# Joining 24 of 32 work units into twelve of 8 MB in an instance-norm kernel

## The chip, the cores and the metric

The kernel runs on one core of a Trainium2 chip. A core has a matrix engine (TensorE, PE), a vector engine (VectorE, DVE), an activation engine (ScalarE, ACT), GpSimd (POOL) and a synchronising engine (SyncE, SP), which run side by side, each in the order of its own instructions. Data moves between the memory outside (HBM) and the on-chip memory (SBUF, 128 partitions) by DMA: an engine issues a transfer on its queue, and 16 DMA engines carry it, each a part of the rows. The metric is the device time of one run in microseconds. Three runs of the kernel before gave 626.78, 626.83 and 626.91 us; the median is 626.83.

## The reference

```python
def reference(x, gamma):            # x: (4, 8, 16, 256, 256) f32, gamma: (8, 16)
    mu = x.mean(axis=(3, 4), keepdims=True)
    var = ((x - mu) ** 2).mean(axis=(3, 4), keepdims=True)
    x_norm = (x - mu) / np.sqrt(var + 1e-5)
    out = x_norm * gamma[None, :, :, None, None]
```

There are 4 x 8 x 16 = 512 channels of 65536 numbers, 134 MB in and as many out. Each channel is normalised by its own mean and variance and scaled by its gamma. The input is read once and the output written once.

## The kernel before

The input is one long run of numbers, cut into 32 units of 4 MB (16 channels each). A unit is a tile of 128 partitions by 8192 numbers; a channel lies in 8 neighbouring partitions (S = 8), and each partition's row of 32 KB is contiguous in HBM. Six slots (AHEAD = 6) of 4 MB hold units; unit u uses slot u % 6.

At the start (L51 to L57) a small store writes into the output ("touch"), gamma is loaded, and six loads are issued: units 1 and 3 on ACT's queue, the others on SP's. Setup then builds, on GpSimd, a 128 x 128 matrix (navg) that sums over the 8 partitions of a channel and divides by -65536, and, with TensorE and VectorE, a column of gammas per unit (g_col).

The loop over units (L104) is unrolled, in this order for each unit:

- L106, VectorE: the sum of each row into st. L107, ScalarE: the square of each element (its output goes to junk) and the sum of the squares into st.
- L115, TensorE: one matmul of navg with the two columns of st, into PSUM: minus the mean and minus the mean square, in each partition of the channel.
- L116 (VectorE), L120 (ScalarE, square root), L124 and L126 (VectorE): the variance, its root, the reciprocal and the scale.
- L135, VectorE: the tile is normalised in place. In unit 0 alone, ScalarE does 3/8 of the row (L132).
- L139, ScalarE's queue: the store of the tile. L141, SP's queue: the load of unit u + 6 into the same slot, which waits until that store has landed.

The order on every queue is the program's order. All stores, and the loads of units 1 and 3, are on ACT's queue (q10 in the profile); all other loads on SP's (q1). The program tracks dependencies by parts of a tile: in unit 0, VectorE and ScalarE write two parts of one tile at the same time.

Of the kernel before, what the change touches and what calls it, by code (L numbers as in the profile page):

```python
# [1 line left out]

# [4 lines left out]

F32 = mybir.dt.float32
U8 = mybir.dt.uint8
ALU = mybir.AluOpType  # L10
ACTF = mybir.ActivationFunctionType
AX = mybir.AxisListType


@with_exitstack
def kernel(
    ctx: ExitStack,
    tc: tile.TileContext,
    x: bass.AP,
    gamma: bass.AP,  # L20
    out: bass.AP,
):
    nc = tc.nc
    B, G, C, H, W = x.shape
    P = nc.NUM_PARTITIONS
    HW = H * W
    n_ch = B * G * C
    S = 8
    K = P // S
    F = HW // S  # L30
    U = n_ch // K
    NG = (G * C) // K
    AHEAD = 6
    assert HW % S == 0 and (G * C) % K == 0

    xv = x.rearrange("b g c h w -> (b g c h w)").rearrange("(u p f) -> u p f", p=P, f=F)
    ov = out.rearrange("b g c h w -> (b g c h w)").rearrange("(u p f) -> u p f", p=P, f=F)
    gv = gamma.rearrange("g c -> (g c)")

    data = ctx.enter_context(tc.tile_pool(name="data", bufs=1))  # L40
    singles = ctx.enter_context(tc.tile_pool(name="singles", bufs=1))
    psum = ctx.enter_context(tc.tile_pool(name="psum", bufs=4, space=bass.MemoryType.PSUM))
    ctx.enter_context(tc.manual_schedule())

    slots = [data.tile([P, F], F32, name=f"xt{i}") for i in range(AHEAD)]

    def load(u, queue):
        queue.dma_start(out=slots[u % AHEAD][:], in_=xv[u])  # L48


    g_row = singles.tile([1, G * C], F32, name="g_row")  # L51
    touch = singles.tile([16, 128], F32, name="touch")
    nc.vector.memset(touch[:], 0.0)  # L53
    nc.gpsimd.dma_start(out=ov[0][0::S, 0:128], in_=touch[:])  # L54
    nc.gpsimd.dma_start(out=g_row[:], in_=gv[None, :])  # L55
    for u in range(AHEAD):
        load(u, nc.scalar if u in (1, 3) else nc.sync)  # L57

    eps_t = singles.tile([P, 1], F32, name="eps_t")
    nc.gpsimd.memset(eps_t[:], 1e-5)  # L60
    one = singles.tile([1, 1], F32, name="one")
    nc.gpsimd.memset(one[:], 1.0)
    navg = singles.tile([P, K, S], F32, name="navg")
    nc.gpsimd.memset(navg[:], -1.0 / HW)  # L64
    nc.gpsimd.affine_select(  # L65
        out=navg[:], in_=navg[:], pattern=[[-S, K], [0, S]], compare_op=ALU.is_ge,
        fill=0.0, base=0, channel_multiplier=1,
    )
    nc.gpsimd.affine_select(  # L69
        out=navg[:], in_=navg[:], pattern=[[S, K], [0, S]], compare_op=ALU.is_ge,  # L70
        fill=0.0, base=S - 1, channel_multiplier=-1,
    )
    navg_w = navg[:].rearrange("p k s -> p (k s)")
    root_eps = singles.tile([P, 1], F32, name="root_eps")
    nc.scalar.activation(out=root_eps[:], in_=eps_t[:], func=ACTF.Sqrt)  # L75
    g_rep = singles.tile([1, NG, K, S], F32, name="g_rep")
    g_ps = psum.tile([P, NG], F32, name="g_ps", bufs=1)
    g_col = singles.tile([P, NG], F32, name="g_col")

    nc.vector.tensor_copy(  # L80
        out=g_rep[:],
        in_=g_row[:].rearrange("o (n k) -> o n k", n=NG).unsqueeze(3).to_broadcast([1, NG, K, S]),
    )
    for n in range(NG):
        nc.tensor.matmul(  # L85
            out=g_ps[:, n : n + 1],
            lhsT=g_rep[:, n].rearrange("o k s -> o (k s)"),
            rhs=one[:],
            start=True, stop=True,
        )  # L90
    nc.vector.tensor_copy(out=g_col[:], in_=g_ps[:])  # L91

    junk = singles.tile([P, F], U8, name="junk")

    st = singles.tile([P, U, 2], F32, name="st")
    nvar = singles.tile([P, U], F32, name="nvar")
    std = singles.tile([P, U], F32, name="std")
    rstd = singles.tile([P, U], F32, name="rstd")
    scale = singles.tile([P, U], F32, name="scale")

    shift = singles.tile([P, 1], F32, name="shift")

    squares = []
    for u in range(U):  # L104
        t = slots[u % AHEAD]
        nc.vector.reduce_sum(out=st[:, u, 0:1], in_=t[:], axis=AX.X)  # L106
        square = nc.scalar.activation(  # L107
            out=junk[:], in_=t[:], func=ACTF.Square, accum_out=st[:, u, 1:2],
        )
        if u:  # L110

            tc.declare_no_dep(square.ins, squares[-1].ins, reason="junk, ordered by the root between")
        squares.append(square)
        ps = psum.tile([P, 2], F32, name="ps")
        nc.tensor.matmul(out=ps[:], lhsT=navg_w, rhs=st[:, u], start=True, stop=True)  # L115
        nc.vector.tensor_scalar(  # L116
            out=nvar[:, u : u + 1], in0=ps[:, 0:1], scalar1=ps[:, 0:1],
            scalar2=ps[:, 1:2], op0=ALU.mult, op1=ALU.add,
        )
        nc.scalar.activation(  # L120
            out=std[:, u : u + 1], in_=nvar[:, u : u + 1], func=ACTF.Sqrt,
            bias=eps_t[:], scale=-1.0,
        )
        nc.vector.reciprocal(out=rstd[:, u : u + 1], in_=std[:, u : u + 1])  # L124
        g = u % NG
        nc.vector.tensor_mul(  # L126
            out=scale[:, u : u + 1], in0=rstd[:, u : u + 1], in1=g_col[:, g : g + 1],
        )
        cut = F * 5 // 8 if u == 0 else F
        if cut < F:  # L130
            nc.vector.tensor_mul(out=shift[:], in0=ps[:, 0:1], in1=scale[:, u : u + 1])  # L131
            nc.scalar.activation(  # L132
                out=t[:, cut:], in_=t[:, cut:], func=ACTF.Identity, bias=shift[:], scale=scale[:, u : u + 1],
            )
        nc.vector.tensor_scalar(  # L135
            out=t[:, :cut], in0=t[:, :cut], scalar1=ps[:, 0:1], scalar2=scale[:, u : u + 1],
            op0=ALU.add, op1=ALU.mult,
        )
        nc.scalar.dma_start(out=ov[u], in_=t[:])  # L139
        if u + AHEAD < U:  # L140
            load(u + AHEAD, nc.sync)  # L141


# [1 line left out]
_INS = ['x', 'gamma']  # L145
_OUTS = [((4, 8, 16, 256, 256), 'float32')]


# [23 lines left out]
```

## Time and profile before

| what | value |
|---|---|
| median of three runs | 626.83 us |
| span of the profiled execution, first to last instruction | 625.2 us (its own device time is not given apart from the span) |
| VectorE busy | 441.8 us, 71% |
| ScalarE busy | 241.8 us, 39% |
| TensorE busy | 21.4 us, 3% |
| HBM traffic | 134.22 MB read, 134.23 MB written, 429 GB/s over the span |
| first load issued / first packet | 0.81 / 1.82 us |
| last load lands | 585.5 us |
| last store issued / landed | 600.6 / 624.3 us |

The page gives the busy time of each engine, the span in 40 slices with the DMA engines' share of busy time, the DMA queues with their packets, and groups of instructions with their mean duration and what ended the idle time before them. A packet is one row's contiguous bytes, or the 4 B that marks a transfer as complete on one DMA engine. Groups are named by line of the kernel, engine, operation and tiles.

### The profile page before, as it was taken

Reading aid. Unit: us, or ns where it says so; the run is one execution under the profiler, and the core shown is the slowest. Engines: PE = TensorE matmul, PEld = TensorE weight load, DVE = VectorE, ACT = ScalarE, POOL = GpSimd, SP = SyncE. Lnnn points to the kernel's source line nnn. Section 1 sums busy time; section 2 is a strip of 40 time slices with the busy share of each in tenths; the row PEclk is TensorE's granted clock in tenths of the full one; section 3 lists DMA queues with packets and bytes.
Section 4 is the critical chain, followed back from the end, with each engine's and each line's share of the span. In section 5 each row is a group of like instructions: output and inputs, shape, how many; then the busy total and the mean of one; then the engine's idle time right before and its main releaser. Section 6 shows DMA issues by size and latency. Waiting matters only on the chain.

```text
span 625.2 us, 635 instructions
## 1 busy us (share of the span) xinstructions
PE 21.4 (3%) x80; PEld 19.5 (3%) x80; DVE 441.8 (71%) x164; ACT 241.8 (39%) x99; POOL 2.4 (0%) x11
## 2 busy tenths in 40 slices
PE   0200000000000000000000000000000000000000
PEld 0200000000000000000000000000000000000000
DVE  0589999998776687666786767867668676687730
ACT  0464444444443244432344423444224442244400
POOL 1000000000000000000000000000000000000000
DMA  8999999999999999999999999999999999999998
GB/s 370 436 407 432 436 436 436 436 436 430 423 436 434 434 428 434 434 436 436 436 436 428 426 436 436 432 430 434 434 436 436 436 436 421 432 436 434 434 430 367
DMA packets 9282, 268.46 MB, mean 429 GB/s; under 512 B 1072, under 2 KB 1088, under 8 KB 1088
## 3 DMA queue, kind: packets, MB, share of 16 engines
q10 hardware_dynamic: 4896, 142.61, 52.9%
q1 hardware_dynamic: 4320, 125.83, 46.8%
q0 software_dynamic: 64, 0.01, 0.0%
q14 instruction: 2, 0.02, 0.0%
HBM read 134.22 MB, written 134.23 MB: 429 GB/s over the span
## 4 chain that ended last, share of the span: by engine, by line
another core or an unknown queue 61%; DMA 17%; DVE 15%; SPq 1%; PE 1%; issue 0%; ACT 0%
DMA xt<-in_x_dram 10%; DVE st L106 10%; DMA out_dram<-xt 8%; DVE xt L135 5%; SPq L48 1%; PE ps L115 1%; ACT std L120 0%; DVE nvar L116 0%; DVE rstd L124 0%; DVE scale L126 0%; DVE shift L131 0%
## 5 line engine op out<-in xcount | busy, mean ns | idle before, releaser
L106 DVE TENSOR_REDUCE st<-xt 128x1 f32<-128x8192 f32 x32 | 277.9, 8684 | 102.2 <-DMA xt<-in_x_dram 102.2
L107 ACT ACTIVATE junk<-xt 128x8192 uint8<-128x8192 f32 x32 | 225.0, 7030 | 272.0 <-DMA xt<-in_x_dram 233.8
L135 DVE TENSOR_SCALAR xt<-xt,ps,scale 128x8192 f32<-128x8192 f32 (+1 forms) x32 | 144.0, 4500 | 1.1
L120 ACT ACTIVATE std<-nvar,eps_t 128x1 f32<-128x1 f32 x32 | 9.4, 295 | 79.4 <-DVE nvar L116 79.4
L115 PE MATMUL ps<-st,navg 128*128 128x2 f32 x64 | 17.8, 348 | 557.3 <-DVE st L106 557.3
L115 PEld LDWEIGHTS ps<-st,navg 128*128 128x128 f32 x64 | 16.0, 310 | 559.1 <-issue 546.2
L116 DVE TENSOR_SCALAR nvar<-ps 128x1 f32<-128x1 f32 x32 | 9.2, 286 | 23.8 <-PE ps L115 23.8
L124 DVE RECIPROCAL rstd<-std 128x1 f32<-128x1 f32 x32 | 5.2, 163 | 11.6 <-ACT std L120 11.6
L80 DVE COPY g_rep<-g_row 1x1024 f32<-1x1024 f32 x1 | 0.7, 681 | 14.4 <-DMA g_row<-in_gamma_dram 14.4
L107 ACT ACTIVATION_READ_ACCUMULATOR junk<-xt 128x1 f32 x32 | 6.0, 186 | 0.0
L126 DVE TENSOR_TENSOR scale<-rstd,g_col 128x1 f32<-128x1 f32 x32 | 5.1, 158 | 1.1
L85 PE MATMUL g_ps<-one,g_rep 1*128 1x1 f32 x16 | 3.5, 347 | 16.3 <-DVE g_rep L80 16.3
L85 PEld LDWEIGHTS g_ps<-one,g_rep 1*128 1x128 f32 x16 | 3.5, 326 | 16.3 <-issue 16.3
L132 ACT ACTIVATE xt<-xt,shift,scale 128x3072 f32<-128x3072 f32 x1 | 2.9, 2947 | 0.7 <-DVE shift L131 0.7
L91 DVE COPY g_col<-g_ps 128x8 f32<-128x8 f32 x1 | 0.2, 167 | 3.7 <-PE g_ps L85 3.7
L75 ACT ACT_TABLE_LOAD x1 | 1.3, 1283 | 1.7 <-PEq L156 1.7
L53 DVE MEMSET touch<- 16x128 f32 x1 | 0.2, 165 | 0.9 <-PEq L156 0.9
L54 POOL DMA_DIRECT2D out_dram<-touch x1 | 0.6, 617 | 0.8 <-DVE touch L53 0.8
L55 POOL DMA_DIRECT2D g_row<-in_gamma_dram x1 | 0.5, 487 | 0.0
L65 POOL TENSOR_SCALAR_AFFINE_SELECT navg<-navg 128x128 f32<-128x128 f32 x1 | 0.4, 400 | 0.1
L69 POOL TENSOR_SCALAR_AFFINE_SELECT navg<-navg 128x128 f32<-128x128 f32 x1 | 0.4, 399 | 0.1
L64 POOL MEMSET navg<- 128x128 f32 x1 | 0.2, 230 | 0.0
(8 smaller groups left out, 1.0 us busy)
## 6 DMA issues: line engine op xcount, KB each, us to landing
out_dram<-xt ACTq DMA_DIRECT2D x32, 4096.0 KB, 62.5
xt<-in_x_dram SPq DMA_DIRECT2D x30, 4096.0 KB, 38.5
xt<-in_x_dram ACTq DMA_DIRECT2D x2, 4096.0 KB, 31.7
out_dram<-touch POOLq DMA_DIRECT2D x1, 8.0 KB, 9.3
g_row<-in_gamma_dram POOLq DMA_DIRECT2D x1, 0.5 KB, 13.5
```

The source lines that it names most:

```text
L48: queue.dma_start(out=slots[u % AHEAD][:], in_=xv[u])
L75: nc.scalar.activation(out=root_eps[:], in_=eps_t[:], func=ACTF.Sqrt)
L85: nc.tensor.matmul(out=g_ps[:, n : n + 1], lhsT=g_rep[:, n].rearrange("o k s -> o (k s)"), rhs=one[:], start=True, stop=True,)
L106: nc.vector.reduce_sum(out=st[:, u, 0:1], in_=t[:], axis=AX.X)
L107: square = nc.scalar.activation(out=junk[:], in_=t[:], func=ACTF.Square, accum_out=st[:, u, 1:2],)
L115: nc.tensor.matmul(out=ps[:], lhsT=navg_w, rhs=st[:, u], start=True, stop=True)
L116: nc.vector.tensor_scalar(out=nvar[:, u : u + 1], in0=ps[:, 0:1], scalar1=ps[:, 0:1], scalar2=ps[:, 1:2], op0=ALU.mult, op1=ALU.add,)
L120: nc.scalar.activation(out=std[:, u : u + 1], in_=nvar[:, u : u + 1], func=ACTF.Sqrt, bias=eps_t[:], scale=-1.0,)
L124: nc.vector.reciprocal(out=rstd[:, u : u + 1], in_=std[:, u : u + 1])
L126: nc.vector.tensor_mul(out=scale[:, u : u + 1], in0=rstd[:, u : u + 1], in1=g_col[:, g : g + 1],)
L132: nc.scalar.activation(out=t[:, cut:], in_=t[:, cut:], func=ACTF.Identity, bias=shift[:], scale=scale[:, u : u + 1],)
L135: nc.vector.tensor_scalar(out=t[:, :cut], in0=t[:, :cut], scalar1=ps[:, 0:1], scalar2=scale[:, u : u + 1], op0=ALU.add, op1=ALU.mult,)
```

## The change

The 32 units become 20: four of 4 MB, twelve of 8 MB, four of 4 MB (sizes, in halves of 4 MB). An 8 MB unit has 128 rows of 64 KB, 32 channels, and a channel lies in 4 partitions (S = 4). The six slots become three tiles of two half-slots each (pairs); an 8 MB unit takes a whole pair, a 4 MB unit a half. The memory taken is the same. Each unit is still loaded by one transfer and stored by one.

An 8 MB unit is summed and squared half by half (two reductions and two squares of 8192 numbers), its two matmuls add up in PSUM, and it is normalised by one instruction over 16384 numbers. There are two averaging matrices and two gamma columns, for S = 8 and S = 4. A load goes out after the store of the last unit that still held part of its place: the loads of units 16 and 17 follow store 13, those of units 18 and 19 follow store 14. The first loads are those of units 0 to 4.

```diff
-    S = 8
-    K = P // S
-    F = HW // S
-    AHEAD = 6
+    F = 8192
+    HALVES = 6
+    ENDS = 4
+    sizes = [1] * ENDS + [2] * ((n_half - 2 * ENDS) // 2) + [1] * ENDS
+    starts = [sum(sizes[:i]) for i in range(len(sizes))]
+    def rows(flat, u):
+        n = sizes[u] * P * F
+        lo = starts[u] * P * F
+        return flat[lo : lo + n].rearrange("(p f) -> p f", p=P)
-    slots = [data.tile([P, F], F32, name=f"xt{i}") for i in range(AHEAD)]
+    pairs = [data.tile([P, 2 * F], F32, name=f"xt{i}") for i in range(HALVES // 2)]
+    def home(u):
+        at = starts[u] % HALVES
+        return pairs[at // 2], (at % 2) * F
     def load(u, queue):
-        queue.dma_start(out=slots[u % AHEAD][:], in_=xv[u])
+        t, c = home(u)
+        src = rows(x_flat, u)
+        n = sizes[u] * F
+        step = n
+        for k in range(0, n, step):
+            queue.dma_start(out=t[:, c + k : c + k + step], in_=src[:, k : k + step])
-    for u in range(AHEAD):
+    first = [u for u in range(len(sizes)) if starts[u] + sizes[u] <= HALVES]
+    for u in first:
         load(u, nc.scalar if u in (1, 3) else nc.sync)
+    for S in (8, 4):
+        K = P // S
+        w = singles.tile([P, K, S], F32, name=f"navg{S}")
...
     for u in range(U):
-        t = slots[u % AHEAD]
-        nc.vector.reduce_sum(out=st[:, u, 0:1], in_=t[:], axis=AX.X)
+        t, c = home(u)
+        S = 8 // sizes[u]
+        halves = range(sizes[u])
+        for h in halves:
+            part = t[:, c + h * F : c + (h + 1) * F]
+            col = starts[u] + h
+            nc.vector.reduce_sum(out=st[:, col, 0:1], in_=part, axis=AX.X)
+            square = nc.scalar.activation(
+                out=junk[:], in_=part, func=ACTF.Square, accum_out=st[:, col, 1:2],
+            )
         ps = psum.tile([P, 2], F32, name="ps")
-        nc.tensor.matmul(out=ps[:], lhsT=navg_w, rhs=st[:, u], start=True, stop=True)
+        for h in halves:
+            nc.tensor.matmul(
+                out=ps[:], lhsT=navg[S], rhs=st[:, starts[u] + h],
+                start=h == 0, stop=h == sizes[u] - 1,
+            )
...
+        step = sizes[u] * F
+        for k in range(0, sizes[u] * F, step):
+            n = min(step, cut - k)
+            nc.vector.tensor_scalar(
+                out=t[:, c + k : c + k + n], in0=t[:, c + k : c + k + n], scalar1=ps[:, 0:1],
+                scalar2=scale[:, u : u + 1], op0=ALU.add, op1=ALU.mult,
+            )
+            nc.scalar.dma_start(out=dst[:, k : k + step], in_=t[:, c + k : c + k + step])
-        if u + AHEAD < U:
-            load(u + AHEAD, nc.sync)
+        for v in range(len(first), U):
+            need = starts[v] + sizes[v] - HALVES
+            if starts[u] < need <= starts[u] + sizes[u]:
+                load(v, nc.sync)
```

## The prediction

> **What bounds the kernel now.** I read the page's slices first, then its queues and issues, then the engines' groups, and last the DMA view of short windows and the chain at the end.
>
> ```profile
> span 625.2 us, 635 instructions
> ...
> DMA  8999999999999999999999999999999999999998
> ...
> DMA packets 9282, 268.46 MB, mean 429 GB/s; under 512 B 1072, under 2 KB 1088, under 8 KB 1088
> ...
> q10 hardware_dynamic: 4896, 142.61, 52.9%
> q1 hardware_dynamic: 4320, 125.83, 46.8%
> ...
> L106 DVE TENSOR_REDUCE st<-xt 128x1 f32<-128x8192 f32 x32 | 277.9, 8684 | 102.2 <-DMA xt<-in_x_dram 102.2
> L107 ACT ACTIVATE junk<-xt 128x8192 uint8<-128x8192 f32 x32 | 225.0, 7030 | 272.0 <-DMA xt<-in_x_dram 233.8
> L135 DVE TENSOR_SCALAR xt<-xt,ps,scale 128x8192 f32<-128x8192 f32 (+1 forms) x32 | 144.0, 4500 | 1.1
> ...
> out_dram<-xt ACTq DMA_DIRECT2D x32, 4096.0 KB, 62.5
> xt<-in_x_dram SPq DMA_DIRECT2D x30, 4096.0 KB, 38.5
> ```
>
> The two data queues fill 99.7% of the 16 DMA engines' time: q1 (SP's, the loads) and q10 (ACT's, all stores and two loads). VectorE, the next busiest, idles 102 us for loads. So only two things change the time: what a packet costs, and whether a DMA engine ever has nothing to do.
>
> Packet starts in the trace price both. On one engine, 32 KB packets start 1209.5 ns apart, a 512 B packet holds the engine 23 ns, a 4 B one (a transfer's completion mark, one per engine) 6 ns. A line through 512 B and 32 KB has 4.5 ns that does not depend on size.
>
> Next, how queues share an engine: the DMA view of a window (7.1 to 9.55 us) in which a small transfer runs on q0.
>
> ```profile
> DMA packets 48, 1.06 MB, mean 431 GB/s; under 512 B 0, under 2 KB 16, under 8 KB 16
> ## 3 DMA queue, kind: packets, MB, share of 16 engines
> q1 hardware_dynamic: 16, 0.52, 49.5%
> q10 hardware_dynamic: 16, 0.52, 49.5%
> q0 software_dynamic: 16, 0.01, 1.1%
> ```
>
> Each queue put through 16 packets, one per engine, though q0's have 512 B and the others 32 KB. The turn is a packet, not a number of bytes; the 4 B marks take turns of their own too. Last, the end of the chain and of the timeline:
>
> ```profile
> 547.05 38.49 DMA xt<-in_x_dram
> ...
> 596.03 4.55 DVE xt L135
> ```
>
> ```profile
> 585.57 8.69 DVE L106 TENSOR_REDUCE st<-xt 128x1 f32<-128x8192 f32 x1 [4.33 <-DMA xt<-in_x_dram]
> ...
> 600.62 0.34 ACTq L139 DMA_DIRECT2D out_dram<-xt  x1
> ```
>
> The last load lands at 585.54. Four stores of 4 MB are then left, 9.66 us each (they land at 595.2, 604.9, 614.6 and 624.3). The last is issued at 600.6, while the one ahead of it still runs until 614: 13 us of cover, and the DMA never stops.
>
> **The change part by part.**
>
> *Packets.* Twelve 8 MB units move 128 rows of 64 KB each way: 8 packets per engine in place of 16. That removes 12 x 2 x 8 = 192 packets per engine, at 4.5 ns: 0.86 us; 24 fewer completion marks at 6 ns: 0.14 us. Gain 1.0 us. A 64 KB packet is then 2 x 1209.5 - 4.5 = 2414.5 ns. No row shows one: bounds are a packet cost of 8 ns (the recorded length of a 32 KB packet, 1213, less its bytes), a gain of 1.7, and none at all. The starts are nearest, so 1.0. The Trainium skill ("DMA: Bandwidth & Descriptors", Why small descriptors are slow) gives some 3 cycles per packet, 3.5 ns at its 850 MHz; an estimate from that page makes the gain 0.8 us, where the trace's row makes it 1.0.
>
> *Issues.* 24 fewer, at 0.33 us on SP and 0.34 on ACT; hidden before (both queues held transfers), so nothing.
>
> *Setup.* A second averaging matrix on GpSimd (a memset and two selects, 0.23 + 0.40 + 0.40 us) ends before 5 us and is needed at 31. The second gamma column adds to VectorE a copy of 512 (at most the 0.68 of the 1024 one) and one of 0.17, to TensorE 4 matmuls at 0.22, with waits some 2 us from 20.06; the first load lands at 22.75. If that cover fails, unit 0 is at most 1 us late, and its store waits behind a load on q10 until about 41 anyway. Nothing.
>
> *Chain of a unit.* From landing to store issue a 4 MB unit takes 15.05 us (585.57 to 600.62). An 8 MB unit starts only when all of it has landed: a second reduction (+8.61) and a normalisation of 16384 in place of 8192 (+4.29, by the slope between the 5120 and 8192 forms, 2.94 and 4.55): 28.0. Squares (2 x 7.2 on ACT) lie beside the reductions; the first half's matmul beside the second's reduction; the second half's costs what the matmul cost before. Per 8 MB that is 28.0 in place of 30.1, so VectorE gains.
>
> *Buffers.* With both queues on 64 KB packets, a transfer takes 8 pairs of turns, 8 x 4.83 = 38.6 us. A pair of half-slots goes through load 38.6, chain 28.0, store 38.6 and about 4 us of marks, landings (0.4) and first packets (1.0 after issue, from 0.81 to 1.82 at the start): 109 of the 3 x 38.6 = 116 us that three pairs allow. Nothing lost in the middle, with 7 us to spare.
>
> *The ends, where sizes mix.* Here a 64 KB packet on one queue alternates with a 32 KB one on the other, 2.41 against 1.21, so the queue with big rows gets two thirds. At the head the big one is a load (unit 4, beside stores 0 and 1): loads run ahead, harmless, since VectorE is at units 0 to 3 until 81. At the tail it is the stores: loads 16 to 19 are small, stores 14 and 15 big. I walked each engine's turns through the program by the rules above (alternate packets, marks a turn, landing 0.4, first packet 1.0 after issue, chains 15.05 and 28.0). For the kernel before the walk gives load 4 at 62.5 (trace 62.4), the last load at 585.3 (585.5) and the span 625.0 (625.2). For the change:
>
> - The load of unit 15 lands at 506.9. Before, 4 loads (of 32) were left at 508; now also 4, so no change so far.
> - Load 16 against store 14: 8 x (2.41 + 1.21) = 29.0 us, to 535.5. Equal packets would have taken 19.4.
> - Store 15 is ready in time (506.9 + 28.0 + 1.0 = 536.0), so load 17 pays the same: to 564.5.
> - Loads 18 and 19 against stores 16 and 17, small on both sides: 19.4 each, to 583.9 and 603.3. The last load is 18 us later than before.
> - Then only stores 18 and 19 are left. Store 18 runs to 613.0. Unit 19 lands at 603.7, its store is issued at 618.75 and starts at 619.7.
>
> The DMA stands idle from 613.0 to 619.7: 6.7 us. What is late is the last unit's chain, whose cover of 13 us is gone. Sum: 625.2 - 1.0 + 6.7 = 630.9 us of span. The median of the three runs, 626.83, lies 1.6 above the span shown (which leaves out launch and end), taken as fixed: **632.5 us**, slower by 0.9%.
>
> The walk steps by packets: if the 8 MB chain takes 29, 30 or 32 us, or first packets take 1.3 to 2.0 us after issue, store 15 comes later, some load packets go unopposed, and the span is 1.2 to 3.6 us lower; tried over these values it lay from 627.2 to 631.7. Random lateness of packets, as in the trace's odd 1.23 to 1.3 us ones near 100 us, adds up to 0.7. With the 0.2 us by which the walk falls short before, and the 1.6, that is 629 to 633.8 for this case's time.
>
> **Rivals.**
>
> *The engines share by bytes once packets differ (not slower).* A 64 KB row might be served as two turns of 32 KB. The place is the tail from 507 on: load 16 takes 19.4, the last load ends at 586.3, the last store is issued at 601.8 with store 18 running to 613, and only the packet gain is left: 626.83 - 1.0 = 625.8. It decides as soon as the last load ends before 596.5 (16.5 ahead of 613.0). Against it: 16 packets of 512 B for 16 of 32 KB. For it: no row shows a packet over 32 KB between two queues.
>
> *The rows are cut into 32 KB pieces (the change does not do what it says).* Then only the marks are saved: 626.7. The trace shows no 64 KB row, so neither for nor against, save that the 32 KB rows went whole.
>
> *Large packets stream more slowly.* Each 1% on a 64 KB packet costs 24 x 19.32 x 0.01 = 4.6 us; with the tail's loss, 637 at 1%; without, 630. For it: the first stores beside loads (40 to 44 us) fell to 369 GB/s; against: all later mixing held 431 to 436. The Trainium skill ("DMA: Bandwidth & Descriptors", Latency and other measured facts, on HBM row pitch at large powers of two) has rates falling as the pitch of rows grows, from 207 GB/s a direction at 512 KiB to 103 at 4 MiB. The change doubles the pitch from 32 to 64 KB, still below its list; no run shown here tests it.
>
> *Three pairs starve the DMA in the middle.* It needs a chain over 37 us where the sum has 28.0; at 40, the walk ends at 639.7, 641 for the median. Nothing in the rows adds 9 us to the chain.
>
> **How the numbers follow.** Alternation at the tail: 0.72, since the sharing rule is shown by three packet sizes but not at 64 KB. Bytes: 0.10. Cut rows: 0.07. Slower packets: 0.06. Starving: 0.05. A difference of 0.2% is 1.25 us, about what a measurement of this kernel tells from none. Of the first, 0.03 could end within it (a long chain), the rest is slower: 0.69 + 0.06 + 0.05 = 0.80. Same: 0.03, cut rows 0.07, and half of bytes (625.8 is just inside 625.58): 0.15. Faster: the rest of bytes, 0.05. The likeliest case's own range is 629 to 633.8 and holds about 0.69; reaching down to cut rows and bytes, at 625.7, takes it to 0.86.
>
> **What would show it.** The page should have 5120 data packets, 640 marks and the 66 others: 5826 in place of 9282 (8898 if rows are cut). Window 510 to 560: q10 moves twice q1's bytes if turns are packets, equal bytes otherwise. The last landing of a load: about 603.7 (586 by bytes). The DMA's slices just before the end: a gap of 5 to 7 us, and the chain of waits ending in the last load, its reduction, its normalisation and its store. Middle slices stay full, and 64 KB packets start 2.41 us apart. The prediction is wrong if q10's share at the tail is one half, if store 15 is late enough to let loads run alone, or if the middle shows gaps.

## The result and the profile after

The changed kernel takes 637.56 us (median of 4 runs, 633.88 to 638.31), the kernel before 626.87 (626.78 to 627.34). The ratio is 1.0157, 95% interval [1.0132, 1.0182]: slower by 1.6%, where 632.5 and slower by 0.9% was forecast, with 633.8 as the upper end. The profiled execution took 638.2 us for a span of 636.5, so 1.7 us lie around the span, as with the kernel before.

The page of the changed kernel, in lines that answer to those shown before:

```profile
span 636.5 us, 556 instructions
...
DMA  9999999999999999999999999999999999999966
GB/s 375 441 404 428 437 404 412 461 416 441 445 408 457 408 449 441 416 449 408 449 416 449 453 408 449 408 449 457 412 449 408 449 428 426 457 395 426 430 289 266
DMA packets 5827, 268.48 MB, mean 422 GB/s; under 512 B 688, under 2 KB 704, under 8 KB 704
...
L135 DVE TENSOR_REDUCE st<-xt 128x1 f32<-128x8192 f32 x32 | 276.8, 8681 | 149.3 <-DMA xt<-in_x_dram 149.3
```

The rows did become packets of 64 KB: 5827 in all, 5826 forecast. VectorE works 11 us less than before (430.8 us busy, 441.8 before) and waits 47 us more for loads (149.3, 102.2 before). Up to the last two slices the DMA engines look full; those two, 289 and 266 GB/s, hold most of the loss. Two stretches of the end, columns as in the profile's table by stretches (start and end, length in us, busy time and instructions of PE, its weight loads, DVE, ACT and POOL, granted clock, DMA share, GB/s; packets are counted where they start, so a share can pass 1):

```profile
613.00:625.00 12.00, 0.56 (x2) 0.50 (x2) 10.30 (x5) 3.87 (x3) 0.00 (x0) 1.00 0.27 113
625.00:635.00 10.00, 0.00 (x0) 0.00 (x0) 0.00 (x0) 0.00 (x0) 0.00 (x0) 1.00 0.98 419
```

The timeline of the same end:

```profile
590.09 8.69 DVE L135 TENSOR_REDUCE st<-xt 128x1 f32<-128x8192 f32 x1 [9.79 <-DMA xt<-in_x_dram]
...
605.15 0.34 ACTq L177 DMA_DIRECT2D out_dram<-xt  x1
609.45 8.69 DVE L135 TENSOR_REDUCE st<-xt 128x1 f32<-128x8192 f32 x1 [4.34 <-DMA xt<-in_x_dram]
...
624.51 0.34 ACTq L177 DMA_DIRECT2D out_dram<-xt  x1
```

The last load lands at 609.4 in place of 585.5. Store 18 is through at 615.8 on most engines, store 19 is issued only at 624.5, and between them the DMA engines stand idle. What holds the loads back shows in the DMA view of a stretch in which small loads run beside big stores (517 to 533 us):

```profile
DMA packets 131, 6.42 MB, mean 401 GB/s; under 512 B 0, under 2 KB 0, under 8 KB 0
## 3 DMA queue, kind: packets, MB, share of 16 engines
q10 hardware_dynamic: 65, 4.26, 62.1%
q1 hardware_dynamic: 66, 2.16, 31.3%
```

As many packets on each queue, twice the bytes on q10: a turn is a packet at 64 KB too.

The account of the loss, mean over the 16 DMA engines, from the packets' starts and lengths:

| | before | after |
|---|---|---|
| packets longer than the usual length of their size, sum of the excess | 1.6 us | 4.5 us |
| idle between packets | 0.1 us | 10.1 us, of which 9.5 in gaps that begin between 600 and 620 |
| last packet ends, mean of the engines | 623.4 us | 635.2 us |

Excess +2.9 and idle +10.0, less 1.0 for fewer packets and marks, make +11.9 against 11.8 measured at the last packets; the span grew by 11.3.

### The profile page after: what moved, and what is told of

Same layout as the page of the kernel before. It is cut to its first block, busy times and chain, and to the rows that moved or that the text cites. A ratio compares the mean times of both kernels' runs of the same rounds, so it can differ in the third digit from the quotient of the medians.

```text
span 636.5 us, 556 instructions
## 1 busy us (share of the span) xinstructions
PE 23.2 (4%) x88; PEld 21.3 (3%) x88; DVE 430.8 (68%) x118; ACT 238.3 (37%) x87; POOL 3.6 (1%) x14
## 2 busy tenths in 40 slices
DMA packets 5827, 268.48 MB, mean 422 GB/s; under 512 B 688, under 2 KB 704, under 8 KB 704
## 4 chain that ended last, share of the span: by engine, by line
DMA 58%; DVE 25%; another core or an unknown queue 12%; PE 1%; issue 0%; ACT 0%; SPq 0%
DMA xt<-in_x_dram 32%; DMA out_dram<-xt 27%; DVE st L135 16%; DVE xt L173 8%; PE ps L144 1%; ACT std L152 0%; DVE nvar L148 0%; DVE rstd L156 0%; DVE scale L159 0%; SPq L64 0%; DVE shift L164 0%
## 5 line engine op out<-in xcount | busy, mean ns | idle before, releaser
L135 DVE TENSOR_REDUCE st<-xt 128x1 f32<-128x8192 f32 x32 | 276.8, 8681 | 149.3 <-DMA xt<-in_x_dram 149.3
L173 DVE TENSOR_SCALAR xt<-xt,ps,scale 128x16384 f32<-128x16384 f32 (+2 forms) x20 | 140.6, 7030 | 0.7
L152 ACT ACTIVATE std<-nvar,eps_t 128x1 f32<-128x1 f32 x20 | 5.9, 295 | 67.1 <-DVE nvar L148 67.1
L148 DVE TENSOR_SCALAR nvar<-ps 128x1 f32<-128x1 f32 x20 | 5.7, 287 | 14.9 <-PE ps L144 14.9
L156 DVE RECIPROCAL rstd<-std 128x1 f32<-128x1 f32 x20 | 3.3, 164 | 7.2 <-ACT std L152 7.2
L109 PE MATMUL g_ps<-one,g_all 1*128 1x1 f32 x24 | 5.4, 347 | 16.8 <-DVE g_all L103 16.8
L109 PEld LDWEIGHTS g_ps<-one,g_all 1*128 1x128 f32 x24 | 5.3, 324 | 16.8 <-issue 16.2
L159 DVE TENSOR_TENSOR scale<-rstd,g_col 128x1 f32<-128x1 f32 x20 | 3.2, 159 | 0.7
## 6 DMA issues: line engine op xcount, KB each, us to landing
xt<-in_x_dram SPq DMA_DIRECT2D x12, 43.5
out_dram<-xt ACTq DMA_DIRECT2D x12, 44.9
```

The lines of the kernel that those rows point to most:

```text
L109: nc.tensor.matmul(out=g_ps[:, n : n + 1], lhsT=g_all[:, n * P : (n + 1) * P], rhs=one[:], start=True, stop=True,)
L135: nc.vector.reduce_sum(out=st[:, col, 0:1], in_=part, axis=AX.X)
L148: nc.vector.tensor_scalar(out=nvar[:, u : u + 1], in0=ps[:, 0:1], scalar1=ps[:, 0:1], scalar2=ps[:, 1:2], op0=ALU.mult, op1=ALU.add,)
L152: nc.scalar.activation(out=std[:, u : u + 1], in_=nvar[:, u : u + 1], func=ACTF.Sqrt, bias=eps_t[:], scale=-1.0,)
L159: nc.vector.tensor_mul(out=scale[:, u : u + 1], in0=rstd[:, u : u + 1], in1=g_col[S][:, g : g + 1],)
L173: nc.vector.tensor_scalar(out=t[:, c + k : c + k + n], in0=t[:, c + k : c + k + n], scalar1=ps[:, 0:1], scalar2=scale[:, u : u + 1], op0=A ...
```

## The experiments

Theory A is the prediction's: turns are packets, and at the tail big stores hold back small loads. Theory B: 64 KB packets are themselves slower and drive the DMA engines apart. Theory C: giving back places by pairs costs by itself. Theory E came up on the way: a load queue that runs empty comes back late and slowly. All kernels were timed beside the kernel before (626.8 to 627.1).

| kernel | median us | ratio to before, 95% interval |
|---|---|---|
| changed kernel | 637.56 | 1.0157 [1.0132, 1.0182] |
| tail32 | 629.82 | 1.0050 [1.0037, 1.0063] |
| cut14 | 631.67 | 1.0073 [1.0058, 1.0087] |
| st32 | 629.34 | 1.0041 [1.0028, 1.0053] |
| even | 630.24 | 1.0055 [1.0041, 1.0069] |
| all32 | 627.45 | 1.0009 [1.0000, 1.0017] |
| all32w | 629.88 | 1.0048 [1.0035, 1.0062] |
| gap32 | 627.12 | 1.0004 [0.9995, 1.0013] |
| swap1 | 628.67 | 1.0034 [1.0012, 1.0056] |
| swapall | 635.80 | 1.0138 [1.0125, 1.0152] |
| ld32t | 652.54 | 1.0409 [1.0376, 1.0443] |
| even2 | 650.86 | 1.0324 [1.0281, 1.0367] |

The median of even2 is that of all its six runs, its ratio that of the four shorter ones (643.5 to 651.9). One of the twelve runs of swap1 took 636.7, the others 627.3 to 629.2.

"Cut" means that an 8 MB transfer is made by two transfers of 4 MB, each with half of every row: packets of 32 KB, the rows of a tile still 64 KB apart in HBM. The normalisation stays one instruction. The units whose transfers are cut are named by two sets:

```diff
-        step = n
+        step = F if u in CUT_LOADS else n
         for k in range(0, n, step):
             queue.dma_start(out=t[:, c + k : c + k + step], in_=src[:, k : k + step])
...
-        step = sizes[u] * F
+        step = F if u in CUT_STORES else sizes[u] * F
         for k in range(0, sizes[u] * F, step):
...
             nc.scalar.dma_start(out=dst[:, k : k + step], in_=t[:, c + k : c + k + step])
```

### The tail: tail32 and cut14

In tail32:

```diff
+    CUT_LOADS = ()
+    CUT_STORES = (14, 15)
```

In cut14:

```diff
+    CUT_LOADS = ()
+    CUT_STORES = (14,)
```

> Only the stores of units 14 and 15 are cut into two transfers of 32 KB rows each (all other 8 MB transfers keep 64 KB rows), so that beside the small loads 16 to 18 both queues have 32 KB packets. Theory A (a turn is a packet, so big-row stores take two thirds of the DMA engines from the small loads at the tail, and the last unit comes too late): the last load lands at 585 to 596 in place of 609, the gap of some 10 us before the last store is gone, median 626 to 629. Theory B (64 KB packets are themselves slower and drive the 16 DMA engines apart, so that every landing waits for the slowest engine): the last load still lands after 600 and the median is 632 or more.

> Of the two big stores beside the small loads only 14 is cut. Theory A: half of the lag at the tail: last load lands at 594 to 603, between 609 (neither cut) and 590 (both), gap of 0 to 4 us, median 629 to 633. If the tail's lag were not made by these two stores, the same as the changed kernel, 636 or more.

With both stores cut, the last load lands at 590.4 (timeline of tail32):

```profile
590.36 8.69 DVE L137 TENSOR_REDUCE st<-xt 128x1 f32<-128x8192 f32 x1 [4.32 <-DMA xt<-in_x_dram]
...
605.42 0.34 ACTq L179 DMA_DIRECT2D out_dram<-xt  x1
```

Beside store 15 (DMA view of tail32, 548 to 564 us) the loads now get their half:

```profile
q1 hardware_dynamic: 124, 3.54, 51.2%
q10 hardware_dynamic: 115, 3.31, 47.9%
```

The idle time falls from 10.1 to 0.3 us, and the median by 7.7 us. With one store cut, the last load lands at 600.9, the idle time is 1.7 us, the median 631.7. The order is as theory A has it: none cut 637.6, one 631.7, both 629.8, and the last load's landing 609.4, 600.9, 590.4. tail32 came out 0.8 us above theory A's range. What is left of it, 3.0 us over the kernel before, is not idle time: in its trace the packets' excess is 1.9 us over that of the kernel before, and the engines' last packets end between 623.4 and 627.3.

These landings are those of the slowest DMA engine, since a transfer has landed when the last of its 16 completion marks has come. On the median engine the last load's mark comes at 596.4, 598.4 and 587.5 (none, one and both cut), and from the first engine to the last it takes 12.9, 3.1 and 2.9 us. So the step from none to one is a step in the spread of the engines, and only cutting both brings the loads of most engines forward.

### The other way round: st32

```diff
+    CUT_LOADS = ()
+    CUT_STORES = range(4, 16)
```

> All stores of 8 MB units are cut into two transfers of 32 KB rows; loads keep 64 KB rows. Theory A: loads now have the larger turn, two thirds of the DMA engines while both queues are busy, so they run ahead, wait for places, and none is late at the end: last load lands at 585 to 596, no gap before the last store, median 626 to 629. Theory B: half of the 64 KB packets are left, so about half of the loss: 631 to 633.

The loads have the larger turn and run ahead: q1 has no packet for 10 to 11.5 us in every round, the last load lands at 581.9, 3.7 us earlier than in the kernel before. The median, 629.3, is 0.3 over theory A's range and well under theory B's. So in these runs it is the small turn on the side of the loads that makes the tail late.

### Packet length, or the release by pairs: all32, even, all32w

In all32:

```diff
+    CUT_LOADS = range(4, 16)
+    CUT_STORES = range(4, 16)
```

In even:

```diff
+    CUT_LOADS = (4, 5)
+    CUT_STORES = (14, 15)
```

all32w is all32 with the halves of a load in the other order, so that the first transfer on SP's queue waits for the later of the two places:

```diff
-        for k in range(0, n, step):
+        for k in reversed(range(0, n, step)):
             queue.dma_start(out=t[:, c + k : c + k + step], in_=src[:, k : k + step])
```

> Every 8 MB transfer is cut into two of 32 KB rows (rows still 64 KB apart in HBM); units, pairs, places and the order of the work stay. A reduction may now begin when the first half of its unit has landed. Theory A: all turns are equal again, the last load lands at 585 to 592, no gap, median 626.5 to 628.5. Theory B, if the distance of 64 KB between rows makes packets slow: packets of 32 KB over 1.25 us by the dozen and median 630 or more. Theory B, if the length of a packet does it: as theory A. Theory C (three pairs in place of six slots is itself what costs): gaps stay, median 632 or more.

> Loads 4 and 5 and stores 14 and 15 are cut into transfers of 32 KB rows, so that 64 KB rows only ever run beside 64 KB rows, save load 6 beside the end of store 3. Theory A: no lag at the tail (last load lands at 585 to 592), and load 4, with half the engines in place of two thirds, takes until about 80, so that SP's queue is hardly empty before load 5 and the slow stretch at 84 to 91 shrinks: median 626 to 628. Theory B: 10 of 12 loads and stores still have 64 KB packets, so 632 or more.

> As the kernel with every 8 MB transfer cut into two of 32 KB rows, but the second half of each load is issued first, so that SP waits for the whole pair to be free, as with one 8 MB load, and the unit's work starts when the later of its halves has landed. Only the packet's length now differs from the changed kernel. If the length of packets is what costs: no drift of the engines (all land within 1.5 us of each other), recorded excess of packets about 1.6 us per engine as before, median 626.8 to 628. If places given back by pairs cost: over 629, with loads stopped for want of a place and the engines drifting.

all32 comes within 0.7 us of the kernel before (excess of 1.6 us per engine, all last packets between 622.9 and 624.4): joined units, matmuls that add up in PSUM and rows 64 KB apart cost next to nothing. But cutting loads also lets the first half of a load go as soon as one half-slot is free. all32w takes that back, with 32 KB packets throughout, and loses 2.4 us: excess 2.8 us, of which 1.4 between 80 and 100, and the engines' last packets spread from 623.8 to 625.6. It is as slow as tail32, 629.88 and 629.82 (its profiled run, 628.74, is the shortest of its five). So a loss of the size that is left over the tail comes without 64 KB packets, against theory B, and goes with the release by pairs, theory C, though with 2.4 us and not by gaps. Two things differ between all32w and all32, and no run here parts them: a load waits for the later of its places, and a unit's work starts only when both of its halves have landed. Both all32w and even missed their ranges for theory A, which had nothing for it. In even the slow stretch didn't shrink but moved, to 120 us, where the load queue first ran empty there.

### An emptied queue in the kernel before: gap32, swap1, swapall

These three change the loop's end in the kernel before. gap32:

```diff
-        if u + AHEAD < U:
-            load(u + AHEAD, nc.sync)
+        for v in {0: (), 1: (), 2: (6, 7, 8)}.get(u, (u + AHEAD,)):
+            if v < U:
+                load(v, nc.sync)
```

swap1, and swapall below it:

```diff
+        for v in {0: (), 1: (7, 6)}.get(u, (u + AHEAD,)):
+            if v < U:
+                load(v, nc.sync)
```

```diff
+        if u % 2 and u + AHEAD < U:
+            load(u + AHEAD, nc.sync)
+            load(u + AHEAD - 1, nc.sync)
```

> The kernel before (32 KB rows, six slots), with loads 6, 7 and 8 all issued after store 2, so that SP's queue is empty for about 10 us from 81 on while stores run alone, as it is from 71 to 86 in the changed kernel. If the slow stretch at 84 to 91 comes with any return of loads after stores alone: 1 to 2 us of excess per engine near 92, median 627.8 to 628.8. If it takes 64 KB packets: no such excess, 626.6 to 627.2.

> The kernel before with one thing changed: loads 7 and 6 are issued in that order after unit 1, so that SP waits for store 1 and its queue runs empty once, from about 81 to 86, while stores run alone. Theory E (a load queue that has run empty comes back late, 4 to 5 us after its issue, and into a stretch of slow packets): excess of 1 to 1.8 us per engine near 85 to 95, median 627.8 to 629. If it takes 64 KB rows, 8 MB units or pairs: excess as before, 626.6 to 627.2.

> The kernel before (4 MB units, 32 KB rows) with all later loads issued two by two, the second first, so that places come back by pairs as in the changed kernel. Theory E: as the kernel with 32 KB rows whose loads wait for the whole pair, 628.5 to 630.5, excess 2.5 to 3.5 us, engines 2 to 4 us apart. If the joined units and not the release by pairs cost there: 626.6 to 627.3.

gap32 did not do what it was made for: SP waits only for the place that a load needs, load 6 went out at 62.7 as soon as store 0 had landed, and the queue was never empty. Its 627.12 tells nothing on theory E.

swap1 did. Load 7 stands first on SP and needs store 1, so it is issued at 82.2; on one DMA engine the last packet of load 5 ends at 80.9 and the next load packet starts at 87.2. The stretch from 82 to 98 us, for the kernel before, swap1 and the changed kernel in turn:

```profile
82.00:98.00 16.00, 0.55 (x2) 0.50 (x2) 14.83 (x6) 8.49 (x4) 0.00 (x0) 1.00 1.02 442
```

```profile
82.00:98.00 16.00, 0.56 (x2) 0.50 (x2) 14.82 (x6) 8.48 (x4) 0.00 (x0) 1.00 1.02 399
```

```profile
82.00:98.00 16.00, 0.56 (x2) 0.50 (x2) 16.00 (x2) 13.60 (x4) 0.00 (x0) 1.00 0.99 383
```

The packets that start in it move 442, 399 and 383 GB/s at a DMA share of about 1: the engines are occupied, their packets take longer. The excess between 80 and 100 us is under 0.1, 1.5 and 1.8 us per engine. swap1 costs 1.6 us in the median (its ratio's interval reaches from 0.1 to 0.6%), in a kernel with 4 MB units and 32 KB rows. That is what theory E expected: one emptying of the load queue goes with the whole of the stretch. swapall has the same stretch (1.3 us) and no second emptying, but its 635.8 is above what was expected (628.5 to 630.5), for another reason: the last load to land is unit 30's, so two chains of 15 us come after it lands at 592.1, and the DMA idles for 8.0 us near the end.

```profile
592.06 8.69 DVE L106 TENSOR_REDUCE st<-xt 128x1 f32<-128x8192 f32 x1 [8.77 <-DMA xt<-in_x_dram]
...
622.05 0.34 ACTq L139 DMA_DIRECT2D out_dram<-xt  x1
```

This timeline of swapall's end shows again how the order of the last landings decides about the cover.

### Small loads beside big stores all along: ld32t and even2

ld32t, with the halves of a load in the order of all32w, and below it even2:

```diff
+    CUT_LOADS = range(4, 16)
+    CUT_STORES = (14, 15)
```

```diff
+    CUT_LOADS = (4, 5, 6)
+    CUT_STORES = (14, 15)
```

> All loads have 32 KB rows (second half issued first), stores of units 4 to 13 keep 64 KB rows, stores 14 and 15 are cut. If slow packets come with long loads: excess about 1.6 us per engine, no drift, median 626 to 627.5. If they come with long packets on either queue: excess of 2.5 to 4, drift of 2 to 4 us, 628.5 to 630. The tail is even, so no idle gap above 1 us in either case.

> Loads 4, 5 and 6 and stores 14 and 15 are cut into transfers of 32 KB rows (first half first), so that SP's queue should hold a transfer until units of 64 KB rows run beside each other in step, and the tail is even. If queues that run empty are the cause of what is left over the tail: little excess, the 0.8 us of packets is gained, median 625.9 to 627. If the queue still empties later, or 64 KB packets drive the engines apart by themselves: 628.5 to 631.

Both are far outside what any theory had (even2 between 643.5 and 655.1 us, ld32t between 647.6 and 655.0). In even2 the stretch from 120 to 190 us, where cut loads run beside 64 KB stores, goes at

```profile
120.00:190.00 70.00, 1.11 (x4) 1.00 (x4) 26.80 (x6) 14.54 (x5) 0.00 (x0) 1.00 1.01 362
```

against 432 in all32 over the same stretch:

```profile
120.00:190.00 70.00, 2.23 (x8) 2.00 (x8) 53.60 (x12) 29.09 (x10) 0.00 (x0) 1.00 1.00 432
```

There half of the 64 KB store packets take 2.8 to 3.2 us, and the longest 3.7, in place of 2.42. The profiled run of even2 took 654.9 us, close to its longest; that of ld32t, 647.6, is the shortest of its six and shows a like loss. In ld32t the excess is 15.6 us per engine, and transfers land with up to 25 us between the first and the last engine. The Trainium skill ("DMA: Bandwidth & Descriptors", Latency and other measured facts) has rates falling with the pitch of rows from 512 KiB up. Rows 64 KB apart alone are not it here: all32 has them on both sides at 432 GB/s. Which meeting of addresses or sizes it is stays open. The changed kernel has no cut loads; where its small loads run beside big stores (500 to 580 us), the excess is 0.6 us per engine.

## Why the prediction was wrong

The direction was right, and a turn is a packet, as forecast. The size was not right: +5.6 us forecast, +10.7 measured, the time 3.8 us over the upper end. Two terms were too small: the idle gap (6.7, measured 10.0) and the slow packets (nothing in the sum and up to 0.7 in the range, measured 2.9 per engine). Behind the gap stands the tail of the walk, which let all 16 DMA engines do the same.

- *Packets.* Right. 64 KB packets start 2414.2 ns apart, 2414.5 forecast: with 1209.4 ns for 32 KB that is 4.6 ns less per joined pair, 192 times, 0.9 us.
- *Turns are packets.* Right where both queues have work: 65 packets against 66, 62% against 31% of the time. The rivals of sharing by bytes and of rows cut into pieces fall with the lines shown for 517 to 533 us, and tail32 shows what the share costs here: 7.7 us. But over the window that the prediction named, 510 to 560, q10 moves only 1.24 times the bytes of q1, not twice:

```profile
q10 hardware_dynamic: 197, 11.86, 55.2%
q1 hardware_dynamic: 340, 9.60, 44.8%
```

- *Chain of a unit.* Right: unit 15 from 514.69 to its store's issue at 542.61, 27.9 us; 28.0 forecast. Setup and issues cost nothing that shows.
- *"Store 15 is ready in time ..., so load 17 pays the same: to 564.5."* This is the step that failed. Store 15 was issued at 542.6 where the walk had 535, and its first packet started at 546.2. On 11 of the 16 engines load 17 had by then run alone, and its completion marks came at 549.1 to 549.4. The prediction had named this as a sign of being wrong. On those engines the last load was through at 596.2 to 596.6, 7 us ahead of the walk's 603.3. One engine was 3.8 us behind them at unit 15. There only half of load 17 ran before store 15, the rest took turns with its 64 KB packets, and the mark came at 564.9, 15.7 us after those of the others. It stayed behind: the marks of the last load lie in the packets of q1 from 596 to 596.8 us (11 marks and one packet of 32 KB) and from 608.6 to 609.4 us (the last mark):

```profile
q1 hardware_dynamic: 12, 0.03, 10.2%
```

```profile
q1 hardware_dynamic: 1, 0.00, 0.1%
```

- *The idle gap.* 6.7 us forecast, 10.0 measured, and not by the way that was forecast. Unit 17 landed at 565.3, close to the walk, by luck: one engine set it. Unit 19 landed at 609.4 for the same reason. Had it landed with the 11 engines, store 19 would have been issued near 612, before store 18 was through at 615.8, and there would have been no gap; without the slowest engine alone (the next mark is at 602.2) the gap would have been some 3 us. Both are estimates from these marks and the chain of 15.05 us. So the gap takes both the share of the turns, which tail32 takes away, and engines that have drifted apart. No run here keeps the share and takes the drift away, and only one run of the changed kernel was profiled.
- *Engines alike, no slow packets.* The slowest engine had 10.4 us of excess where most had 3.8. Landings were spread over some 4 us from 320 to 515 us (1.0 in the kernel before).
- *First packet 1.0 after issue.* Right only for idle engines (store 19: 624.51 to 625.45 on one of them). Beside a busy queue a load's first packet started 3.5 to 5.6 us after its issue in nearly every round (load 15: 471.29 to 475.69), and a store's 4.2 us (store 15: 542.61 to 546.81 on one engine). Issue to landing takes 43.5 and 44.9 us (medians of loads and stores of 8 MB), which with the chain of 28.0 uses up the 116 us of three pairs: the 7 us to spare were not there. Unit 15 came at 514.7 where the walk had 506.9: of these 7.8 us, 3.0 lie in the issue of its load and 4.8 in the transfer. By itself this does not make the kernel slower: the prediction's rules worked again with 4.4 us in place of 1.0, all engines alike, give an estimate of 598 for the last load and 628 for the span.
- *"At the head ... loads run ahead, harmless".* Load 4 does land at 71.7 (72.1 by the prediction's rules), because its packets take two thirds. Load 5 needs the places of both unit 0 and unit 1, so SP's queue is empty until store 1 has landed at 81.4; so far this is as in the walk. But its first packet starts 4.8 us after the issue (on one engine 81.44 to 86.21), and a stretch of slow packets from 84 to 91 comes with it, 1.8 of the 2.9 us. Load 5 lands at 117.7, where the rules give 112.0.
- *"Nothing lost in the middle".* Right for the DMA's time, not for its use. By 580 us an engine of the kernel before has moved 255 load and 222 store pieces of 32 KB, one of the changed kernel 248 and 227 on average: 2 pieces, some 2.3 us, fewer in all, but 7 loads behind and 5 stores ahead. Stores that are early save nothing at the end; loads that are late cost their chain.
- *Rival of slower packets.* Half right. Packets were slower, 2.9 us per engine in sum, but swap1 and all32w have about half of it with 32 KB packets (1.5 and 1.3 us over the kernel before). Why the first return of loads is slow, and the later returns (the changed kernel's q1 empties about a dozen times) are not, stays open, as does whether 64 KB packets add to the engines' drift.

No kernel tried here beat the one before. The 1.0 us that fewer packets and marks save shows in the spacing of the packets, but no kernel with 64 KB rows tried here had it without a larger loss elsewhere.

## What to carry to other kernels

In a kernel that fills its DMA engines, sum what each queue has moved by a given time, not only what all have: work that goes from loads to stores is invisible in the DMA's share, and can come due as an uncovered last chain. Look also at how far apart the DMA engines finish a transfer, since the slowest one sets its landing: here 3.8 us of lag grew to 15.7 us within one load at the tail. Queues share an engine packet by packet, so the longer rows get the larger share: before rows are made longer on one side of a phase, ask which side can afford to be late. Joining buffers in pairs also joins their release, and a load queue that runs empty even once can cost more (here 1.5 us) than all the packet overhead that is saved (1.0 us).

## What was unexpected of the hardware

- A transfer issued on an empty queue starts 0.9 us after its issue on idle DMA engines, but some 3.5 to 6.4 us after it beside a busy queue (4.8 and 4.2 on one engine of the changed kernel, 3.6 to 3.9 at the earliest in most rounds of st32, 5.1 and 6.4 on two engines in swap1).
- The first return of loads after stores had run alone was slow, 1.3 to 1.8 us of excess in sum per engine (mean of the engines; swap1, swapall, all32w, changed kernel), with 32 KB and 64 KB packets alike. A like stretch, some 0.8 us, stands in every one of these kernels and in the kernel before at 38 to 42 us, where the first stores join the loads.
- 64 KB store packets took up to 3.7 us beside loads of 32 KB pieces from rows 64 KB apart (even2), and mostly 2.42 beside 64 KB loads.
